# Output weights and bonus rows laid out for one-piece loads; the even layer's output projection in 256-token tiles with two sets of mixed inputs

## The chip, the cores and the metric

The kernel runs on one core of a Trainium2 chip. The metric is device microseconds (us) of one execution of the whole program; the profile is of one further execution. A core has five engines that run side by side and meet through semaphores: TensorE (PE in the profile, with its weight loads as PEld), VectorE (DVE), ScalarE (ACT), GpSimd (POOL) and SyncE (SP). SP issues all of this kernel's DMA transfers, in the order in which they stand in its instruction stream; the data are moved by the core's 16 DMA engines.

## The reference

A four-branch encoder trunk of one even and one odd layer, applied to a prompt of 1024 tokens and a sample of 2048 tokens, in float32. What matters here is the end of each layer:

```python
def even_layer(x, p):
    proj = rms_norm(x, p['norm']) @ p['w_in']
    u, z_s5, h_rw, z_rw = jnp.split(proj, [...], axis=-1)
    ya = s5_branch(u, z_s5, p)          # 512 columns, gated by silu(z_s5)
    yb = rwkv_branch(h_rw, z_rw, p)     # 512 columns
    return x + jnp.concatenate([ya, yb], -1) @ p['w_out']   # 1024 x 1024

def rwkv_branch(h, z, p):
    ...                                  # y: two scans, summed
    y = (y - mean) * rsqrt(var + RW_LN_EPS) * ln_g + ln_b   # per head of 64
    bonus = sum(r * k * r_k, -1, keepdims=True) * v         # per head of 64
    return (y + bonus) * silu(z)

def odd_layer(x, p):                     # windowed attention, gated
    return x + attn_branch(rms_norm(x, p['norm']) @ p['w_in'], p) @ p['w_out']
```

## The kernel before

The program has five stages, one after the other in time. `input_u` (to about 500 us) and `input_rkv` with `s5` (to about 1110 us) make the branch inputs; `input_rkv` also computes the bonus term and stores it to the DRAM tile `bon`. The recurrent mixers run to about 2270 us. Then one group of three phases follows: `even_out` (mixing, normalising and gating the two branches, the output projection, and x1 = x + result), `odd_in` (the odd layer's input projections) and `attention` (with the odd layer's output projection).

**even_out.** Work is in tiles of TT tokens: 256, 256, 512 for the prompt and four times 512 for the sample, seven tiles. The 1024 mixed inputs of a tile are eight blocks of 128 features. Blocks 0 to 3 are the S5 branch: `mix` (from DRAM tile `s5`) times the gate `zs`. Blocks 4 to 7 are the RWKV branch: per 128 tokens `yf` and `yr` are loaded (DRAM `y`), added, normalised; then for b = 0 to 3 the block is transposed by TensorE into PSUM `pt`, the bonus piece `bo` is loaded from `bon`, and two VectorE operations form (pt * ln_g + bo + ln_b) * zr. `emit` splits each block into a rounded part `mh[k]` (ScalarE) and a remainder `ml[k]` (VectorE). There is one set of `mh`/`ml` (pool `eom`, one buffer each), so a block of the next tile is written only after the projection of this tile has read it. The projection runs per 128 tokens and 512 output columns: 24 matmuls (8 blocks, three products each) into one PSUM buffer; then x is added and x1 stored. `bo` has two buffers, so the pieces for b = 2, 3 are asked for when those for b = 0, 1 have been used.

**Where the narrow shapes are.** `bon` is stored as [4, 2, 64, L], and a piece for b is `bon[2*(b%2):+2, 1-b//2, :, t0:t0+TT]`: two groups of 64 rows, whose DRAM side has the dimensions 2 x 64 x TT. The last four of the eight row blocks of `ev_w_out`, and all 16 pieces of `od_w_out` (eight row blocks, two column halves), are 2 x 64 rows of the weight in the same way. The SBUF side has 128 partitions each time.

**Order.** In this group, and in the two input groups, the code's operations are recorded with all their dependences (`Program.note`) and put into each engine's stream by a planner (`Program.put`): it keeps a clock for each engine, gives every operation a cost (a DMA by its bytes alone), and takes next what could start first, by rank. So a change of sizes or of the number of DMAs changes the order on every engine. All recorded operations carry line L412 in the profile; they are told apart by their operands: `ps<-sb` are the projections (also those of other phases of these groups), `ps<-ident,sb` are transposes, `sb<-bon` are the loads of bonus pieces, `x<-sb` the stores of x1. The mixers between have an order of their own.

Of the kernel before, what the change touches and what calls it, by code (L numbers as in the profile page):

```python
# [470 lines left out]
class Kern:  # L471
# [11 lines left out]
    T1, WP = 256, 2  # L483
# [214 lines left out]
    def input_rkv(self, st):  # L698
# [32 lines left out]
        for s, L in enumerate(self.L):  # L731
            t = self.sp[s]
            for t0 in range(0, L, self.seg):
# [37 lines left out]
                for p in range(4):  # L771
# [48 lines left out]
                    nc.sync.dma_start(t["bon"][p].rearrange("h r l -> (h r) l")[:, o0:o1], v)  # L820
# [916 lines left out]
    def even_out(self, st):  # L1737
        tc, nc, ins = self.tc, self.nc, self.ins
        cp = st.enter_context(tc.tile_pool(name="eoc", bufs=1))
        wo = ins["ev_w_out"][0]  # L1740

        turned_rows = lambda a: a.rearrange("(b h r) c -> h b r c", h=2, r=64)
        rows = [wo[P * k:P * k + P] for k in range(4)] + [turned_rows(wo[512:D])[1 - b // 2, 2 * (b % 2):2 * (b % 2) + 2] for b in range(4)]
# [3 lines left out]
        mp = st.enter_context(tc.tile_pool(name="eom", bufs=1))  # L1747
# [7 lines left out]
        for s, L in enumerate(self.L):  # L1755
            t = self.sp[s]
            sizes = [self.T1] * (512 // self.T1) if s == 0 else []
            sizes += [512] * (L // 512 - (s == 0))
            for t0, TT in zip(itertools.accumulate([0] + sizes), sizes):
                mh = [mp.tile([P, 512], F32R, name=f"mh{k}")[:, :TT] for k in range(8)]  # L1760
                ml = [mp.tile([P, 512], F32R, name=f"ml{k}")[:, :TT] for k in range(8)]
                zs, zr = (lp.tile([P, 4, 4, P], F32, name="z")[:, :TT // P] for _ in range(2))
                mix = [lp.tile([P, 4, 256], F32, name="mix") for _ in range(TT // 256)]
                for i in range(TT // 256):
                    nc.sync.dma_start(mix[i], t["s5"][t0 // 256 + i].rearrange("m c t -> c m t"))
# [8 lines left out]
                for m in range(4):  # L1774
                    out = mp.tile([P, 512], F32, name="smix", bufs=2)[:, :TT]
# [9 lines left out]
                for i in range(TT // P):  # L1785
# [11 lines left out]
                    yq = lp.tile([P, 512], F32, name="bo").rearrange("t (u v) -> t u v", v=64)  # L1797
# [93 lines left out]
    def attention(self, st):  # L1891
# [201 lines left out]
    def build(self):  # L2093
        tc = self.tc
        with ExitStack() as root:
# [14 lines left out]
          "rw_w_up", "rw_a0", "rw_a_up", "rw_k_k", "rw_k_a", "rw_r_k", "rw_ln_g", "rw_ln_b", "ev_w_out", "od_norm",  # L2110
          "od_w_in", "at_q_norm", "at_k_norm", "at_sink", "od_w_out"]


def _layout(inputs):
# [33 lines left out]
```

## Time and profile before

| | us |
|---|---|
| median of 3 runs | 4215.14 |
| lowest and highest | 4213.9 and 4220.34 |
| the profiled execution | 4222.45 |
| its span, first to last instruction | 4220.7 |
| even_out, from the end of the mixers to the last x1 | about 2270 to 2700 |
| PE busy over the whole span | 3795.9 (90%) |
| DVE busy | 2819.6 (67%) |
| ACT, POOL busy | 1933.0 (46%), 1611.2 (38%) |
| DMA: bytes moved | 570.30 MB, mean 135 GB/s |

The profiled execution is 7.3 us above the median. Busy shares are means over stages that differ, and matmuls are pipelined, so a busy PE need not be at its peak; the stage in which the change lies is read by itself. "PEclk" is the clock that TensorE was granted, as a part of 2.4 GHz (1.00 is 2.4 GHz, 0.50 is 1.2 GHz). The "DMA share" of a stretch is the mean over 16 DMA engines. In the chain of waits a piece named DMA is the time in which the last needed thing was a transfer.

### The profile page before, as it was taken

To read this page: it belongs to the slowest core of one execution; us is meant where nothing else is said; L and a number is where in the kernel's file an instruction comes from. 1 tells how busy PE (TensorE), PEld (TensorE's weight loads), DVE (VectorE), ACT (ScalarE), POOL (GpSimd) and SP (SyncE) were. 2 spreads that over 40 slices of the span, in tenths; PEclk is the share of its full clock that TensorE was granted. 3 is DMA by queue.
4 is the path that set the end of the run, shared out by engine and by line. 5 is a ranking of instruction groups with operands and counts; after the bars stand their busy time and mean duration, and the time that the engine had idled before them with its cause. 6 is when DMAs were issued, how large, how long until landed. Compare 5 with 4: busy or idle time off the path is not lost.

```text
span 4220.7 us, 87574 instructions
## 1 busy us (share of the span) xinstructions
PE 3795.9 (90%) x34128; PEld 3138.8 (74%) x34128; DVE 2819.6 (67%) x5513; ACT 1933.0 (46%) x4807; POOL 1611.2 (38%) x2007
## 2 busy tenths in 40 slices
PE   6878999999899999999996688899999979999999
PEld 4756766676788788888764466789999957878877
DVE  7356655656578888889873565444444449999997
ACT  3334333333345555656653111232333337777776
POOL 4422322222464554555511232122222225555554
PEclk9989999999999999999997789999999989999999
DMA  5576566656533343333443554444444422222221
GB/s 159 148 187 211 163 193 184 182 166 192 176 128 112 112 130 115 109 115 118 122 97 105 179 175 170 167 147 158 155 150 140 143 90 70 76 79 78 78 65 59
DMA packets 530946, 570.30 MB, mean 135 GB/s; under 512 B 92066, under 2 KB 430114, under 8 KB 519268
## 3 DMA queue, kind: packets, MB, share of 16 engines
q1 hardware_dynamic: 530532, 564.71, 43.6%
q8 instruction: 268, 4.39, 0.4%
q14 instruction: 146, 1.20, 0.1%
HBM read 398.03 MB, written 166.56 MB: 134 GB/s over the span
## 4 chain that ended last, share of the span: by engine, by line
PE 51%; DVE 16%; DMA 10%; issue 4%; POOL 3%; ACT 2%; SPq 1%; DVEq 0%; ACTq 0%; POOLq 0%
PE ps L412 36%; DVE sb L412 12%; PE acc L886 5%; DMA sb<-bon 3%; ACT sb L412 2%; PE pc L1332 2%; PE acc L969 2%; DMA sb<-wsp 2%; PE pg L1185 2%; POOL lt L1164 1%; DMA sb<-in_od_w_out 1%; DMA rk<-rk 1%; PE pY L1355 1%; PE pc L1319 1%; PE pc L1310 1%
## 5 line engine op out<-in xcount | busy, mean ns | idle before, releaser
L412 PE MATMUL ps<-sb 128*128 128x512 f32 (+8 forms) x12464 | 2563.8, 360 | 245.1 <-ACT sb L412 115.0
L412 PEld LDWEIGHTS ps<-sb 128*128 128x128 f32 (+2 forms) x12464 | 1975.6, 188 | 656.3 <-ACT sb L412 133.4
L412 POOL TENSOR_TENSOR sb<-sb,sb 128x384 f32<-128x384 f32 (+4 forms) x468 | 470.3, 1022 | 435.8 <-ACT sb L412 242.0
L412 POOL TENSOR_TENSOR sb<-sb 128x512 f32<-128x512 f32 (+5 forms) x358 | 316.4, 888 | 808.2 <-ACT sb L412 337.4
L412 DVE TENSOR_TENSOR sb<-ps,sb 128x512 fp32r<-128x512 f32 (+4 forms) x620 | 401.9, 661 | 226.3 <-PE ps L412 135.4
L412 ACT ACTIVATE sb<-sb 128x4 f32<-128x4 f32 (+7 forms) x352 | 269.4, 768 | 482.8 <-DVE sb L412 162.1
L412 POOL TENSOR_TENSOR sb<-sb,mhalf 128x8 f32<-128x8 f32 (+3 forms) x156 | 221.5, 1421 | 687.1 <-DVE sb L412 685.9
L886 PE MATMUL acc<-h,w 128*128 128x128 f32 x3072 | 450.4, 291 | 14.0 <-DMA w<-in_ev_w_zr 13.1
L886 PEld LDWEIGHTS acc<-h,w 128*128 128x128 f32 x3072 | 385.3, 197 | 39.5 <-POOL rt L1279 13.4
L412 PE MATMUL ps<-ident,sb 128*128 128x128 f32 x1888 | 316.0, 280 | 98.2 <-DVE sb L412 94.9
L412 ACT COPY sb<-ps 128x512 f32<-128x512 f32 (+4 forms) x402 | 194.9, 502 | 433.9 <-PE ps L412 419.3
L412 PEld LDWEIGHTS ps<-ident,sb 128*128 128x128 f32 x1888 | 236.8, 144 | 163.2 <-DVE sb L412 117.4
L412 DVE TENSOR_TENSOR sb<-sb,sb 128x512 fp32r<-128x512 f32 (+6 forms) x219 | 263.3, 1208 | 129.0 <-ACT sb L412 105.0
L412 ACT ACTIVATE sb<-sb,sb 128x384 f32<-128x384 f32 (+3 forms) x486 | 299.3, 619 | 108.8 <-DVE sb L412 58.4
L1164 POOL TENSOR_TENSOR lt<-rk,lb 64x256 f32<-64x256 f32 x288 | 216.2, 759 | 192.8 <-PE pY L1355 82.5
L1324 ACT COPY rt<-pc 32x128 f32<-32x128 f32 x768 | 196.8, 256 | 97.3 <-PE pc L1319 86.1
L412 DVE CUSTOM_DVE_ANT_0 sb<-ps,sb,sb 128x384 f32<-128x384 f32 (+1 forms) x384 | 215.4, 587 | 28.5 <-PE ps L412 25.3
L412 ACT ACTIVATE sb<-ps 128x512 f32<-128x512 f32 x108 | 64.4, 596 | 363.9 <-PE ps L412 355.4
L412 ACT CAST sb<-ps 128x512 fp32r<-128x512 f32 x368 | 202.0, 587 | 60.3 <-PE ps L412 57.5
L1149 POOL TENSOR_TENSOR kb<-rk,f 128x128 f32<-128x128 f32 x384 | 197.8, 547 | 82.5 <-PE pg L1195 68.8
L1339 DVE TENSOR_TENSOR rt<-pc,wc 64x256 f32<-64x256 f32 x376 | 158.3, 421 | 70.0 <-PE pc L1333 35.0
L412 DVE SCALAR_TENSOR_TENSOR sb<-sb,sb 128x512 f32<-128x512 f32 (+5 forms) x154 | 126.1, 826 | 117.0 <-ACT sb L412 112.8
(121 smaller groups left out, 4748.9 us busy)
## 6 DMA issues: line engine op xcount, KB each, us to landing
sb<-wsp SPq DMA_DIRECT2D x65, 1024.0 KB
rk<-rk SPq DMA_DIRECT2D x96, 512.0 KB
sb<-in_od_w_in SPq DMA_DIRECT2D x36, 1024.0 KB
h<-h SPq DMA_DIRECT2D x48, 512.0 KB
sb<-in_od_w_z SPq DMA_DIRECT2D x24, 1024.0 KB
qkv<-sb SPq DMA_DIRECT2D x72, 256.0 KB
sb<-qkv SPq DMA_DIRECT2D x72, 256.0 KB
sb<-in_x_sample SPq DMA_DIRECT2D x32, 512.0 KB
```

What stands on the lines that cost most here:

```text
L412: self.ops.append((eng, self.cost(eng, op, outs[-1] if outs[-1] is not k.get("accum_out") else outs[0], ins, a, k), deps, self.rank, lambd ...
L886: nc.tensor.matmul(sums[n][1][:, m * P:m * P + P], w[:, k, m * P:m * P + P], acts[n][0][:, k], start=k == 0, stop=k == KT - 1)
L969: nc.tensor.matmul(ps[:, 256 * (m % 2):256 * (m % 2) + 256], uw_at(k)[:, m], act_at(n)[:, 2 * k:2 * k + 2], start=k == 0, stop=k == 3)
L1149: nc.gpsimd.tensor_tensor(kb[:, sl, :, x, :], arr[n][:, sl, cs], f1[:, sl, cs, a:a + 32], MULT)
L1164: (nc.gpsimd if eng == "POOL" else nc.vector).tensor_tensor(ltv[:, :, :, at:at + 32], arr[n][rows, :, cs], f2[rows, :, cs, off:off + 32], ...
L1185: nc.tensor.matmul(g[64:P, c1, p], kb[0:64, p, c1].rearrange("c s i -> c (s i)"), lt[0:64, c1, 4 + p, 0:64], start=True, stop=True)
L1310: nc.tensor.matmul(pu[32 * q:32 * q + 32, j, :], lt[:, c1, u, 0:32], rt[:, c1, u, :], start=True, stop=True)
L1319: nc.tensor.matmul(pu[rows, 2 + j, :], win["tt"][d][0][rows, sys, :], u1[rows, j, :], start=True, stop=True, tile_position=(32 * q, 32 * q))
L1324: nc.scalar.copy(rt[rows, c1, 2 * q:2 * q + 2, :], pu[rows, 2:4])
L1332: nc.tensor.matmul(pu[0:64, 4 + p, :], lt[:, c1, 4 + p, 64:P], rt[:, c1, 4 + p, :], start=True, stop=True)
L1339: nc.vector.tensor_tensor(nrt[rows, n4 % 2, 4 - 4 * o:8 - 4 * o, :], pu[rows, 4:8], nh["wc"][rows, :, n4:n4 + 1].broadcast_to([64, 4, 64]) ...
L1355: nc.tensor.matmul(pY[32 * q:32 * q + 32, j, :], lt[:, c1, u, 32:64], rt[:, c1, u, :], start=True, stop=True)
```

## The change

The layouts that are made before the program runs now hold the two output weights with their rows in the order in which the kernel reads them (`ev_w_ot`, `od_w_ot`), so each block of 128 rows is one plain [128, columns] piece. `bon` becomes [2, 4, 64, L]; a loaded piece is then 128 rows with one stride, and a store of 128 rows becomes two stores of 64. In `even_out` every tile has 256 tokens (12 tiles), `mh` and `ml` have two buffers of 256 tokens where they had one of 512, the S5 mixing of a block is one VectorE operation on 256 tokens where it was one per 128, and the squares of the normalisation have a buffer `yq` of their own where they shared `bo`'s.

```diff
-            t["bon"] = dp.tile([4, 2, 64, L], F32, name=f"bon{s}")
+            t["bon"] = dp.tile([2, 4, 64, L], F32, name=f"bon{s}")
...
-                    nc.sync.dma_start(t["bon"][p].rearrange("h r l -> (h r) l")[:, o0:o1], v)
+                    for e in range(2):
+                        nc.sync.dma_start(t["bon"][e, p, :, o0:o1], v[64 * e:64 * e + 64])
...
     def even_out(self, st):
-        rows = [wo[P * k:P * k + P] for k in range(4)] + [turned_rows(wo[512:D])[1 - b // 2, 2 * (b % 2):2 * (b % 2) + 2] for b in range(4)]
+        rows = [ins["ev_w_ot"][P * k:P * k + P] for k in range(8)]
...
-        mp = st.enter_context(tc.tile_pool(name="eom", bufs=1))
+        mp = st.enter_context(tc.tile_pool(name="eom", bufs=2))
...
-            sizes = [self.T1] * (512 // self.T1) if s == 0 else []
-            sizes += [512] * (L // 512 - (s == 0))
-            for t0, TT in zip(itertools.accumulate([0] + sizes), sizes):
-                mh = [mp.tile([P, 512], F32R, name=f"mh{k}")[:, :TT] for k in range(8)]
-                ml = [mp.tile([P, 512], F32R, name=f"ml{k}")[:, :TT] for k in range(8)]
-                zs, zr = (lp.tile([P, 4, 4, P], F32, name="z")[:, :TT // P] for _ in range(2))
-                mix = [lp.tile([P, 4, 256], F32, name="mix") for _ in range(TT // 256)]
-                for i in range(TT // 256):
-                    nc.sync.dma_start(mix[i], t["s5"][t0 // 256 + i].rearrange("m c t -> c m t"))
+            TT = 256
+            for t0 in range(0, L, TT):
+                mh = [mp.tile([P, TT], F32R, name=f"mh{k}") for k in range(8)]
+                ml = [mp.tile([P, TT], F32R, name=f"ml{k}") for k in range(8)]
+                zs, zr = (lp.tile([P, TT // P, 4, P], F32, name=n) for n in ("zs", "zr"))
+                mix = lp.tile([P, 4, 256], F32, name="mix")
+                nc.sync.dma_start(mix, t["s5"][t0 // 256].rearrange("m c t -> c m t"))
...
-                    for i in range(TT // P):
-                        nat = lambda a: a.rearrange("c (n j) -> c j n", j=8)
-                        nc.vector.scalar_tensor_tensor(out=nat(out[:, P * i:P * i + P]), in0=mix[i // 2][:, m].rearrange("c (j n) -> c j n", j=8)[:, :, 16 * (i % 2):16 * (i % 2) + 16],
-                                                       scalar=0.25, in1=nat(zs[:, i, m]), op0=MULT, op1=MULT)
+                    nat = lambda a: a.rearrange("c i (n j) -> c i n j", j=8)
+                    nc.vector.scalar_tensor_tensor(out=nat(out.rearrange("c (i t) -> c i t", t=P)), in0=mix[:, m].rearrange("c (j i n) -> c i n j", j=8, i=2),
+                                                   scalar=0.25, in1=nat(zs[:, :, m]), op0=MULT, op1=MULT)
...
-                    yq = lp.tile([P, 512], F32, name="bo").rearrange("t (u v) -> t u v", v=64)
+                    yq = lp.tile([P, 8, 64], F32, name="yq")
...
-                    nc.sync.dma_start(bo, t["bon"][2 * (b % 2):2 * (b % 2) + 2, 1 - b // 2, :, t0:t0 + TT])
+                    nc.sync.dma_start(bo, t["bon"][1 - b // 2, 2 * (b % 2):2 * (b % 2) + 2, :, t0:t0 + TT].rearrange("b r l -> (b r) l"))
...
     # attention, weights(c)
-            v = ins["od_w_out"][0].rearrange("(k e g r) c -> k g e r c", e=2, g=4, r=64)
-            rows = [v[b // 4, b % 4] for b in range(8)]
+            rows = [ins["od_w_ot"][P * b:P * b + P, 512 * c:512 * c + 512] for b in range(8)]
```

Three places show how the instructions move. The first is SP at the start of `even_out`: the loads of the first tile and of the weights. Before:

```order
L412 DMA sb1_24256<-in_ev_w_out 128x1024 x3
L412 DMA sb1_24256<-y0_1_1_99 128x512
L412 DMA sb1_24256<-in_ev_w_out 128x1024
L412 DMA sb1_24256<-y0_0_2_92 128x512
L412 DMA sb1_24256<-y0_0_3_93 128x512
L412 DMA sb1_24256<-bon0_85 128x1x256
L412 DMA sb1_24256<-in_ev_w_out 128x1x1024 x4
L412 DMA sb1_24256<-y0_1_2_100 128x512
L412 DMA sb1_24256<-bon0_85 128x1x256
```

And now:

```order
L412 DMA sb1_24280<-bon0_85 128x256 x2
L412 DMA sb1_24280<-in_ev_w_ot 128x1024 x2
L412 DMA sb1_24280<-y0_0_2_92 128x512
L412 DMA sb1_24280<-y0_1_1_99 128x512
L412 DMA sb1_24280<-in_ev_w_ot 128x1024 x3
L412 DMA sb1_24280<-y0_0_3_93 128x512
L412 DMA sb1_24280<-in_ev_w_ot 128x1024
L412 DMA sb1_24280<-y0_1_2_100 128x512
L412 DMA sb1_24280<-in_ev_w_ot 128x1024 x2
```

The first two bonus pieces now stand ahead of the weights; none of the eight weight pieces is of the 2 x 64 form.

The second is PE in the steady part of `even_out`: `ps0` and `ps1` take the transposes of the RWKV blocks, `ps2` to `ps5` are the accumulators of the projection. Before, from the first transposes of a 512-token tile:

```order
L412 MATMUL ps0_24261<-ident_60,sb1_24256 128x128 x4
L412 MATMUL ps1_24262<-ident_60,sb1_24256 128x128 x4
L412 MATMUL ps2_24263<-sb2_24257 128x512 x6
L412 MATMUL ps0_24261<-ident_60,sb1_24256 128x128 x4
L412 MATMUL ps2_24263<-sb2_24257 128x512
L412 MATMUL ps1_24262<-ident_60,sb1_24256 128x128 x4
L412 MATMUL ps2_24263<-sb2_24257 128x512 x6
L412 MATMUL ps3_24264<-sb2_24257 128x512 x2
L412 MATMUL ps2_24263<-sb2_24257 128x512 x5
L412 MATMUL ps3_24264<-sb2_24257 128x512 x16
L412 MATMUL ps4_24265<-sb2_24257 128x512 x13
L412 MATMUL ps2_24263<-sb2_24257 128x512
```

And now, from the first transposes of a 256-token tile:

```order
L412 MATMUL ps0_24285<-ident_60,sb1_24280 128x128 x2
L412 MATMUL ps1_24286<-ident_60,sb1_24280 128x128 x2
L412 MATMUL ps2_24287<-sb2_24281 128x512 x5
L412 MATMUL ps0_24285<-ident_60,sb1_24280 128x128 x2
L412 MATMUL ps2_24287<-sb2_24281 128x512
L412 MATMUL ps1_24286<-ident_60,sb1_24280 128x128 x2
L412 MATMUL ps2_24287<-sb2_24281 128x512 x12
L412 MATMUL ps3_24288<-sb2_24281 128x512 x17
L412 MATMUL ps2_24287<-sb2_24281 128x512
L412 MATMUL ps3_24288<-sb2_24281 128x512 x2
L412 MATMUL ps4_24289<-sb2_24281 128x512
L412 MATMUL ps2_24287<-sb2_24281 128x512 x5
```

Between the last transposes of a tile and the first matmul that needs its seventh block (the single `ps2` row after the long ones) stood 42 matmuls, and stand 29 now.

The third is SP in the same steady part, around the second pair of bonus pieces of a tile. Before:

```order
L412 DMA sb1_24256<-zs1_2_195 128x2048
L412 DMA sb1_24256<-bon1_144 128x1x512 x2
L412 DMA sb1_24256<-in_x_sample 128x1024
L412 DMA sb1_24256<-y1_0_9_162 128x512
L412 DMA sb1_24256<-y1_0_10_163 128x512
L412 DMA sb1_24256<-y1_0_11_164 128x512
L412 DMA sb1_24256<-y1_0_12_165 128x512
L412 DMA sb1_24256<-zr1_2_191 128x2048
```

And now:

```order
L412 DMA x11_3_200<-sb1_24280 128x1024
L412 DMA sb1_24280<-y1_0_9_162 128x512
L412 DMA sb1_24280<-y1_0_10_163 128x512
L412 DMA sb1_24280<-bon1_144 128x256 x2
L412 DMA sb1_24280<-in_x_sample 128x1024
L412 DMA sb1_24280<-y1_1_10_179 128x512
L412 DMA sb1_24280<-zr1_2_191 128x1024
L412 DMA sb1_24280<-bon1_144 128x256 x2
```

The pair stands behind a store of x1 and two loads of y, and the next tile's first pair follows three loads later.

## Rows read from the trace of the kernel before

**Rows 1.** The page's part 4: the chain that ended last, shares by line

```profile
PE ps L412 36%; DVE sb L412 12%; PE acc L886 5%; DMA sb<-bon 3%; ACT sb L412 2%; PE pc L1332 2%; PE acc L969 2%; DMA sb<-wsp 2%; PE pg L1185 2%; POOL lt L1164 1%; DMA sb<-in_od_w_out 1%; DMA rk<-rk 1%; PE pY L1355 1%; PE pc L1319 1%; PE pc L1310 1%
```

**Rows 2.** Windows: stretch and us, each engine's busy time, PEclk, DMA share, GB/s

```profile
2270.00:2364.00 94.00, 31.28 (x110) 23.95 (x111) 33.55 (x62) 15.39 (x24) 16.14 (x27) 0.64 0.43 145
2364.00:2700.00 336.00, 272.05 (x1146) 217.41 (x1145) 185.92 (x334) 48.31 (x75) 89.66 (x66) 0.89 0.53 178
2700.00:3420.00 720.00, 701.09 (x4772) 650.85 (x4771) 312.77 (x388) 232.85 (x276) 179.17 (x143) 0.99 0.45 147
```

**Rows 3.** Windows: three short stretches of even_out, the columns of Rows 2

```profile
2280.00:2290.00 10.00, 3.87 (x9) 3.10 (x10) 7.62 (x16) 4.88 (x8) 3.79 (x3) 0.50 0.92 337
2310.00:2320.00 10.00, 0.69 (x2) 0.29 (x2) 1.83 (x2) 1.06 (x1) 0.00 (x0) 0.50 0.13 52
2491.07:2549.37 58.30, 48.11 (x209) 38.82 (x209) 33.73 (x61) 7.60 (x13) 17.02 (x13) 0.91 0.53 181
```

**Rows 4.** Timeline: start, us, engine; weight loads of even_out and their rounding

```profile
2284.89 0.38 SPq L412 DMA_DIRECT2D sb<-in_ev_w_out  x1
...
2288.88 22.94 SPq L412 DMA_DIRECT2D sb<-in_ev_w_out  x4
...
2290.72 1.06 ACT L412 ACTIVATE sb<-sb 128x1024 fp32r<-128x1024 f32 x1 [1.61 <-DMA sb<-in_ev_w_out]
...
2305.25 1.06 ACT L412 ACTIVATE sb<-sb 128x1024 fp32r<-128x1024 f32 x1 [8.86 <-DMA sb<-in_ev_w_out]
...
2336.59 1.06 ACT L412 ACTIVATE sb<-sb 128x1024 fp32r<-128x1024 f32 x1 [9.95 <-DMA sb<-in_ev_w_out]
```

**Rows 5.** Chain of waits: start, us, what; pieces in even_out

```profile
2321.77 18.95 DMA sb<-bon
...
2363.48 4.66 DMA sb<-y
...
2471.99 16.80 DMA sb<-bon
...
2491.07 30.19 PE ps L412 x122
...
2549.37 30.08 PE ps L412 x122
```

**Rows 6.** Timeline of one wait for a second pair of bonus pieces

```profile
2469.65 9.82 PE L412 MATMUL ps<-sb 128*128 128x512 f32 x42
...
2471.33 1.98 SPq L412 DMA_DIRECT2D sb<-bon  x2
...
2488.89 0.75 DVE L412 SCALAR_TENSOR_TENSOR sb<-ps,sb,sb 128x512 f32<-128x512 f32 x1 [4.88 <-DMA sb<-bon]
...
2491.07 34.94 PE L412 MATMUL ps<-sb 128*128 128x512 f32 x143 [11.60 <-ACT sb L412]
```

**Rows 7.** Timeline of PE: the first transposes of odd_in's first and second tile

```profile
2699.43 1.03 PE L412 MATMUL ps<-ident,sb 128*128 128x128 f32 x8
...
2835.49 1.03 PE L412 MATMUL ps<-ident,sb 128*128 128x128 f32 x8
```

**Rows 8.** Chain of waits: start of odd_in, and start of attention

```profile
2706.97 12.64 DMA sb<-in_od_w_out
...
3422.49 10.04 DMA sb<-in_od_w_out
...
3434.59 9.67 DMA z<-sb
3444.27 6.55 DMA sb<-qkv
...
3461.92 3.57 PE ps L412 x19
```

**Rows 9.** Tile bon: issue durations on SP, ns min/median/max

```profile
L412 SPq DMA_DIRECT2D bon<-sb x24: 319/332/469, 300.4 to 1107.6; - x24
```

**Rows 10.** The page's part 6: the split weights of the RWKV inputs, count and KB

```profile
sb<-wsp SPq DMA_DIRECT2D x65, 1024.0 KB
```

More of the change, by code (lines that the diff above doesn't have):

```diff
@@ L482 @@
     YF, YR = 5, 1
-    T1, WP = 256, 2
+    WP = 2
     RS, RW, RA = 10, 0, 0
@@ L1739, in even_out @@
         cp = st.enter_context(tc.tile_pool(name="eoc", bufs=1))
-        wo = ins["ev_w_out"][0]
-        turned_rows = lambda a: a.rearrange("(b h r) c -> h b r c", h=2, r=64)
-        rows = [wo[P * k:P * k + P] for k in range(4)] + [turned_rows(wo[512:D])[1 - b // 2, 2 * (b % 2):2 * (b % 2) + 2] for b in range(4)]
+        rows = [ins["ev_w_ot"][P * k:P * k + P] for k in range(8)]
         ln = cp.tile([P, 8], F32, name="ln")
@@ L1774, in even_out @@
                 for m in range(4):
-                    out = mp.tile([P, 512], F32, name="smix", bufs=2)[:, :TT]
-                    for i in range(TT // P):
-                        nat = lambda a: a.rearrange("c (n j) -> c j n", j=8)
-                        nc.vector.scalar_tensor_tensor(out=nat(out[:, P * i:P * i + P]), in0=mix[i // 2][:, m].rearrange("c (j n) -> c j n", j=8)[:, :, 16 * (i % 2):16 * (i % 2) + 16],
-                                                       scalar=0.25, in1=nat(zs[:, i, m]), op0=MULT, op1=MULT)
+                    out = mp.tile([P, TT], F32, name="smix")
+                    nat = lambda a: a.rearrange("c i (n j) -> c i n j", j=8)
+                    nc.vector.scalar_tensor_tensor(out=nat(out.rearrange("c (i t) -> c i t", t=P)), in0=mix[:, m].rearrange("c (j i n) -> c i n j", j=8, i=2),
+                                                   scalar=0.25, in1=nat(zs[:, :, m]), op0=MULT, op1=MULT)
                     emit(m, out)
@@ L1805, in even_out @@
                 for b in range(4):
-                    pt = pst.tile([P, 512], F32, name="pt")[:, :TT]
+                    pt = pst.tile([P, TT], F32, name="pt")
                     for i, y in enumerate(yn):
                         nc.tensor.transpose(pt[:, i * P:(i + 1) * P], y[:, b * P:(b + 1) * P], self.ident)
-                    bo = lp.tile([P, 512], F32, name="bo")[:, :TT]
-                    nc.sync.dma_start(bo, t["bon"][2 * (b % 2):2 * (b % 2) + 2, 1 - b // 2, :, t0:t0 + TT])
+                    bo = lp.tile([P, TT], F32, name="bo")
+                    nc.sync.dma_start(bo, t["bon"][1 - b // 2, 2 * (b % 2):2 * (b % 2) + 2, :, t0:t0 + TT].rearrange("b r l -> (b r) l"))
                     nc.vector.scalar_tensor_tensor(out=bo, in0=pt, scalar=lng[:, b:b + 1], in1=bo, op0=MULT, op1=ADD)
@@ L1907, in weights @@
         def weights(c):
-            v = ins["od_w_out"][0].rearrange("(k e g r) c -> k g e r c", e=2, g=4, r=64)
-            rows = [v[b // 4, b % 4] for b in range(8)]
-            return self.load_rows(cp, lp, [r[:, :, 512 * c:512 * c + 512] for r in rows], f"wo{c}", 0.5, (["wr"], 512, 2))
+            rows = [ins["od_w_ot"][P * b:P * b + P, 512 * c:512 * c + 512] for b in range(8)]
+            return self.load_rows(cp, lp, rows, f"wo{c}", 0.5, (["wr"], 512, 2))
         w = [weights(0)]
@@ L2109 @@
 _PLAIN = ["x_prompt", "x_sample", "ev_norm", "ev_w_in", "s5_log_dt", "s5_glu_w", "s5_glu_b", "rw_mu", "rw_w0",
-          "rw_w_up", "rw_a0", "rw_a_up", "rw_k_k", "rw_k_a", "rw_r_k", "rw_ln_g", "rw_ln_b", "ev_w_out", "od_norm",
-          "od_w_in", "at_q_norm", "at_k_norm", "at_sink", "od_w_out"]
+          "rw_w_up", "rw_a0", "rw_a_up", "rw_k_k", "rw_k_a", "rw_r_k", "rw_ln_g", "rw_ln_b", "od_norm",
+          "od_w_in", "at_q_norm", "at_k_norm", "at_sink"]
 def _layout(inputs):
@@ L2122, in _layout @@
     a["od_w_z"] = np.ascontiguousarray(np.asarray(inputs["od_w_in"])[0][:, 1536:].reshape(D, 2, 2, 4, 64).transpose(0, 1, 3, 2, 4).reshape(D, 1024))
+    wo = np.asarray(inputs["ev_w_out"])[0]
+    a["ev_w_ot"] = np.ascontiguousarray(np.concatenate([wo[:512], wo[512:].reshape(4, 2, 64, D).transpose(1, 0, 2, 3)[::-1].reshape(512, D)]))
+    a["od_w_ot"] = np.ascontiguousarray(np.asarray(inputs["od_w_out"])[0].reshape(2, 2, 4, 64, D).transpose(0, 2, 1, 3, 4).reshape(D, D))
     ln = [np.asarray(inputs[n])[0].reshape(2, 2, 2, 64)[:, :, ::-1] for n in ("rw_ln_g", "rw_ln_b")]
```

## The prediction

> **What bounds the kernel now.** I read the chain of waits by line first: TensorE's own rows lead it everywhere, but loads of the bonus pieces hold 3% of the span (some 125 us) and those of the odd output weight 1% [rows 1]. Both lie in places the change touches, so I cut the span there. From 2364 to 2700 us, the body of even_out, PE is busy 272.05 of 336 us at a granted clock of 0.89, and in the 94 us ahead of it 31.28 us at 0.64; odd_in after it runs at 701.09 of 720 and 0.99 [rows 2]. So even_out is where PE waits, and odd_in is full.
>
> For what it waits, the short stretches say. In 2280 to 2290 us the DMA engines move 337 GB/s at a share of 0.92; in 2310 to 2320 us only 52 GB/s at 0.13, which is two engines of 16, while nothing else is wanted but the four weight pieces of the 2 x 64 form [rows 3]. SP sits 22.94 us in issuing those four, and ScalarE rounds them one by one, from 2305.25 to 2336.59 us three intervals of 10.4 us [rows 4]. That is 512 KB by two engines. The bonus pieces have the same form. In the steady tile of 512 tokens PE runs out of work and stands 11.60 us, because the second pair of pieces, asked for at 2471.33, is first used up to its last piece at 2488.89 [rows 6]; the chain has 16.80 us for it, and one tile later PE starts again, 58.3 us on [rows 5]. In those 58.3 us PE is busy 48.11, VectorE 33.73, GpSimd 17.02, ScalarE 7.60 [rows 3]: no engine is full, the two DMA engines decide, and the clock (0.91, so part of the tile at 1.2 GHz) falls behind each wait.
>
> **The change part by part.** All durations are of the profiled execution (4222.45 us; its span is 4220.7), which is 7.3 us above the median.
>
> Start of even_out (window 2270 to 2364). The fourth weight piece, of the plain form, was issued at 2284.89 and rounded at 2290.72, 5.8 us later under full load [rows 4]. Plain, the other four move in 1.6 us each at 337 GB/s [rows 3]; the raw pieces have four buffers, so the last two wait for a rounding (1.06 us on ScalarE, about as much on VectorE) and another 5.8 us. From 2290.72 I add one such round, 8 us, and 2 us for the order: the last piece is rounded at about 2301 where it was at 2336.59, 35 us earlier. From there to the start of the y load at 2363.48, which follows the first tile's last store, took 27 us with two bonus waits in it (the longer one 18.95 us in the chain, begun earlier [rows 5]). With pieces that land as the 256 KB of y did, 4.66 us [rows 5], I allow 14: the pair 4.7 and its arithmetic 2.2, then 24 matmuls at half clock. Gain 35 + 13 = 48 us; bounds 35 (only the weights) and 55.
>
> Body of even_out. The matmuls stay: 192 per 512 tokens, and 16 transposes. At full clock 42 matmuls took 9.82 us [rows 6], 0.234 each, and eight transposes 1.03 us [rows 7]. A 256-token tile is 96 x 0.234 + 8 x 0.129 = 23.5 us of PE. What hides the rest: with two sets of mixed inputs the S5 blocks of the next tile are made while this one is projected. The RWKV blocks are not ahead by much: in the new order a tile's second pair of bonus pieces is still loaded under its own matmuls, and 29 of them cover it, 6.8 us, where 42 did (9.82). From landing to PE's restart took 2.18 us (2488.89 to 2491.07 [rows 6]); the issue came 1.2 us after the transposes or so (the pieces are half as wide now). So 6.8 - 1.2 - 2.2 = 3.4 us are left for landing. A plain piece of this size isn't in the trace: above it is the 4.66 us of y's 256 KB, below the 128 KB at 337 GB/s, 0.4 us; I take 4.66, since a 512 KB store and two y loads stand just ahead of the pair on SP. So each tile still waits 1.2 us: 24.7 us. The eleven tiles from 2364 to 2700 then take 272, and I add 5 for the second tile, whose order is not yet the steady one: 277 against 336, a gain of 59. Bounds: 11 x 23.5 = 258 with no wait (gain 78), and 11 x 28 with a landing of 8 us (gain 28).
> Does another engine stand in the way? VectorE's operations per 512 tokens go from 60 or so to 68: eight of the 128-token mixings merge, sixteen wider ones split in two. At its mean of 33.73/61 = 0.55 us the eight more make 38.1 us at most, of 49.4. The merged mixing reads `mix` with a larger stride than any row here; were it twice as slow per element, 4 x 0.5 us per tile would still fit. The bytes stay: 181 GB/s x 58.3 us is 10.6 MB per 512 tokens, in 49.4 us 214 GB/s, under the 337 seen [rows 3].
> The Trainium skill, "DMA: Bandwidth & Descriptors", section "Rules for kernel authors", speaks against the smaller tiles: it asks for transfers of 1 MiB or more and for few, large ones. In this trace 337 GB/s came with pieces of 256 and 512 KB [rows 3], and two engines limited, not the count; by its fixed cost of about 2 us a transfer (section "Anatomy of one DMA", given there for the GpSimd path) the 30 more transfers of even_out would be an estimated 60 us of latency, all of it in the way only if none overlapped. The sum above charges only the pair that is seen to be waited for.
>
> Start of odd_in. Its first tile takes 2699.43 to 2835.49, 136.1 us [rows 7]; the five others end at about 3422, 117.4 each. In the surplus of 18.7 us the chain names the odd output weight, 12.64 us [rows 8], which the same two engines carry beside x. The first tile also waits for its own weights and x1, which stay. I take 10; bounds 0 and 19.
>
> Start of attention. From 3422.49 to 3461.92 the chain is od_w_out 10.04, then a store of z 9.67 and a load of qkv 6.55 that stand behind it [rows 8]. Those three make 26.3 us; at 4.66 us each they would make 14.0, so 12.3 us less. I take 13, since the narrow pieces just before them go too; bounds 5 and 20.
>
> Stores of the bonus. 24 become 48, each 0.332 us of SP [rows 9], 8 us in all over some 800 us, among waits of SP. I cost them at nothing: the loads are issued ahead of their use. If that cover is gone they cost 8. The planner also makes a new order of the input stage around them; I take 0, from -8 to +8.
> The same section of the Trainium skill says of two transfers to disjoint partition halves: "Don't bother", use one 128-partition transfer. Here the halves go to different rows of `bon` for the sake of the load. No run shows the pair yet; by the rule the second store is pure extra, and at its 2 us this would be an estimated 48 us if each were waited for. No store of `bon` is among the lines of the chain [rows 1].
>
> Sum: 48 + 59 + 10 + 13 = 130. 4222.45 - 130 = 4092 for the profiled execution, 4085 on the median's footing; I forecast 4085. What is late next is PE itself in even_out, as in odd_in.
>
> **The rivals.**
> First: the second pair still holds every tile. It stands behind 512 KB of x1 and 512 KB of y, 3 us at 337 GB/s, so it may land after 9 us and not 4.66. Then each tile waits 5.6 us and takes 29.1: eleven take 320, the body gains 16, the sum is 87: 4128. For it: y's 4.66 us has no bytes listed ahead of it; against it: in the new order the store is issued early in the tile, before the pair's buffers are free.
> Second: the volume is the bound, not the two engines. If even_out can't pass the 181 GB/s of the steady tile [rows 3], the body gains nothing and the sum is 71: 4144. The 337 GB/s of the first stretch speaks against it.
> Third: the number of transfers. Twenty more bonus loads (28 become 48), each waited for at 4.66 us, give back 93: net 37, 4178. It would need each pair in turn to be late; the chain now shows mainly second pairs.
> Fourth: the loads stay narrow, so the change doesn't do what it says. Then the covers of 29 matmuls make each wait longer and the start stays: about as before, 4215. The new shapes in the order, 128x256 where 128x1x256 stood, speak against it.
> Fifth, slower: the input stage. Its 65 loads of split weights, 1 MB each [rows 10], hold 2% of the chain [rows 1], 84 us; SP's order there is planned anew round 24 more stores. If each of these loads comes 2.5 us later at a point where PE waits for it, that is +163 against -130: 4248. It decides from 2.0 us per load. Against it: 0.33 us of issue per store [rows 9].
>
> **How the numbers follow.** Forecast 0.70, first rival 0.12, second 0.06, third 0.04, fourth 0.03, fifth 0.03, and 0.02 for smaller mixtures that stay faster. The forecast's own terms span gains of 60 (35 + 28 + 0 + 5 - 8) to 180 (55 + 78 + 19 + 20 + 8), but hardly all at one end: 95 to 165 is likely, 4050 to 4120. I extend it to the first rival and a little over, 4140, and leave out the second to fifth: 4050 to 4140. A measurement of this kernel can tell 0.2%, 8 us, from no change. Faster by more than that: all but the fourth and fifth, 0.94; within it: the fourth, 0.03; slower: the fifth, 0.03.
>
> **What would show it.** In the new profile the rounding of even_out's weights should end near 2301 us on the old scale and no stretch of even_out should stand at 0.13 DMA share; bonus loads should leave the front of the chain; PE should restart every 25 us at a granted clock near 1.00, with x1's last store some 105 us earlier; odd_in's first tile should take about 126 us, and attention begin about 27 us after odd_in. Wrong would be: tiles of 28 us or more with a wait on `sb<-bon` in each (first rival), GB/s that stays at 180 with DMA share near 0.9 (second), or an input stage that ends later than 1107 us by tens (fifth).

## The result and the profile after

| us | before | after |
|---|---|---|
| median, 4 runs each | 4217.74 | 4063.43 |
| lowest and highest | 4213.9 to 4223.13 | 4061.16 to 4065.39 |
| profiled execution (span) | 4222.45 (4220.7) | 4065.39 (4063.7) |

The ratio of after to before is 0.9633, interval 0.9616 to 0.965: 154 us faster. The forecast was 4085, with a range of 4050 to 4140.

The chain of waits of after, by line, against [rows 1]:

```profile
PE ps L412 30%; DVE sb L412 11%; PE acc L887 5%; PE pc L1333 2%; PE acc L970 2%; PE pg L1186 2%; ACT sb L412 2%; DMA rk<-rk 1%; DVE ng L1251 1%; DVE z L1253 1%; PE pY L1356 1%; PE pc L1320 1%; POOL lt L1165 1%; PE pc L1311 1%; DVE lt L1206 1%
```

The bonus loads (3%) and the odd output weight (1%) are gone from the leading lines. So are the split weights `sb<-wsp` (2%), but that is no gain: PE's waits on them between 300 and 1100 us are 23.2 us in both profiles. For the stages I cut each profile at the same four events. A runs from even_out's first issue on SP to the second x1 store of its first 256 tokens, B from there to odd_in's first transposes, C to those of odd_in's second tile, and the rest to the end of the span.

| profile | A begins | A | B | C | rest |
|---|---|---|---|---|---|
| before | 2272.8 | 91.5 | 335.1 | 136.1 | 1385.2 |
| after | 2272.0 | 46.8 | 260.5 | 117.0 | 1367.4 |
| difference | -0.8 | -44.7 | -74.6 | -19.1 | -17.8 |

Windows of after (stretch and us; busy time of PE, PEld, DVE, ACT, POOL; granted clock, DMA share, GB/s), against [rows 2, 3]:

```profile
2272.00:2318.80 46.80, 30.30 (x119) 23.06 (x119) 37.78 (x60) 16.12 (x27) 19.89 (x28) 0.78 0.90 309
2318.80:2579.30 260.50, 251.93 (x1131) 204.05 (x1130) 180.89 (x367) 54.78 (x113) 87.96 (x65) 0.99 0.68 230
2280.00:2290.00 10.00, 4.13 (x12) 3.33 (x13) 8.83 (x14) 4.95 (x8) 5.03 (x4) 0.56 1.01 380
2290.00:2300.00 10.00, 9.07 (x42) 7.01 (x40) 9.54 (x11) 5.94 (x7) 6.47 (x4) 1.00 0.86 284
2300.00:2310.00 10.00, 8.34 (x30) 5.80 (x29) 9.93 (x20) 3.21 (x9) 1.26 (x1) 0.83 0.94 325
```

The body of even_out is now full of TensorE work, 251.93 of 260.50 us, at a clock of 0.99 where it was 0.89, and at 230 GB/s where it was 178. In A the mean DMA share is 0.90; the stretch at 0.13 is gone, and of all stretches of 10 us from 2270 to 2580 us none has a share under 0.40.

PE's waits in B, by what ended them (us in total, times, the longest), of before and then of after:

```profile
PE ps L412 <- ACT sb L412: 57.0, 8, 11.6
PE ps L412 <- DVE sb L412: 7.0, 9, 3.5
```

```profile
PE ps L412 <- DVE sb L412: 4.5, 2, 2.8
PE ps L412 <- ACT sb L412: 4.0, 7, 0.7
```

ScalarE is only the last link there: it rounds the block that waited for a bonus piece. The waits fell from 64.0 to 8.5 us, 55.5 less. The rest of B's gain, some 19 us, is PE's own busy time, 271.21 us in the same cut of before, for the same matmuls at the higher clock. The end of before's wait of 11.60 us ([rows 6]) and what came behind it, in the columns of the windows, shows both:

```profile
2486.00:2488.00 2.00, 0.00 (x0) 0.00 (x0) 0.00 (x0) 0.00 (x0) 0.00 (x0) 0.50 0.13 51
2488.00:2490.00 2.00, 0.00 (x0) 0.00 (x0) 1.11 (x2) 0.00 (x0) 0.00 (x0) 0.50 0.13 51
2491.07:2495.00 3.93, 3.92 (x9) 2.77 (x10) 3.93 (x7) 1.25 (x2) 1.02 (x1) 0.50 0.76 272
2500.00:2505.00 5.00, 5.00 (x24) 4.13 (x23) 3.38 (x7) 0.63 (x1) 4.12 (x4) 1.00 0.45 156
```

The wait ends at two engines' share and 51 GB/s. Then PE does 9 matmuls in 3.92 us at a granted clock of 0.50, and 24 in 5.00 us once it is at 1.00. A wait for data was thus paid twice, as idle time and as clock.

ScalarE's roundings of the weights (start, us), against [rows 4]:

```profile
2290.58 1.06 ACT L412 ACTIVATE sb<-sb 128x1024 fp32r<-128x1024 f32 x1 [0.23 <-DMA sb<-in_ev_w_ot]
...
2295.99 1.06 ACT L412 ACTIVATE sb<-sb 128x1024 fp32r<-128x1024 f32 x1 [0.77 <-DMA sb<-in_ev_w_ot]
...
2299.07 1.06 ACT L412 ACTIVATE sb<-sb 128x1024 fp32r<-128x1024 f32 x1 [2.01 <-DMA sb<-in_ev_w_ot]
```

The last begins at 2299.07, where it began at 2336.59. One wait for a second pair, in the timeline (SP, PE and VectorE), against [rows 6]:

```profile
2488.73 6.85 PE L412 MATMUL ps<-sb 128*128 128x512 f32 x29
...
2489.81 0.86 SPq L412 DMA_DIRECT2D sb<-bon  x2
...
2493.94 0.48 DVE L412 SCALAR_TENSOR_TENSOR sb<-ps,sb,sb 128x256 f32<-128x256 f32 x1 [3.89 <-DMA sb<-bon]
2494.75 0.48 DVE L412 SCALAR_TENSOR_TENSOR sb<-ps,sb,sb 128x256 f32<-128x256 f32 x1 [0.33 <-DMA sb<-bon]
...
2496.13 14.13 PE L412 MATMUL ps<-sb 128*128 128x512 f32 x61 [0.55 <-ACT sb L412]
```

The 29 matmuls of the new order cover the pair, and PE stands 0.55 us instead of 11.60. The chain of waits there, against [rows 5]:

```profile
2466.46 4.63 DMA sb<-bon
...
2472.57 9.38 PE ps L412 x40
...
2490.24 4.42 DMA sb<-bon
...
2496.13 9.38 PE ps L412 x40
...
2513.66 3.95 DMA sb<-bon
...
2519.08 60.84 PE ps L412 x276
```

Bonus pieces are still on the chain of the body, seven of them at 2.46 to 4.63 us where one was 16.80, and none behind the last one shown. PE restarts after 23.56 us (2472.57 to 2496.13) and 22.95 (to 2519.08). Odd_in's first tile, against [rows 7], takes 117.0 us:

```profile
2579.31 1.03 PE L412 MATMUL ps<-ident,sb 128*128 128x128 f32 x8
...
2696.31 1.03 PE L412 MATMUL ps<-ident,sb 128*128 128x128 f32 x8
```

At the start of attention, PE's waits in 145 us (before 3415 to 3560, after 3280 to 3425), of before and then of after:

```profile
PE ps L412 <- ACT sb L412: 14.5, 3, 13.6
PE ps L412 <- POOL sb L412: 12.9, 3, 10.9
PE ps L412 <- DVE sb L412: 10.3, 17, 1.4
```

```profile
PE ps L412 <- DVE sb L412: 11.5, 21, 2.1
PE ps L412 <- ACT sb L412: 1.6, 1, 1.6
PE ps L412 <- POOL sb L412: 1.5, 2, 0.8
```

The two long waits, behind the transfers of [rows 8], are gone: 37.7 us became 14.6.

### The profile page after: what moved, and what is told of

It is laid out like the page before. It is cut to its first block, busy times and chain, and to the rows that moved or that the text cites. A ratio compares the mean times of both kernels' runs of the same rounds, so it can differ in the third digit from the quotient of the medians.

```text
span 4063.7 us, 87721 instructions
## 1 busy us (share of the span) xinstructions
PE 3763.6 (93%) x34128; PEld 3118.4 (77%) x34128; DVE 2821.8 (69%) x5545; ACT 1939.8 (48%) x4847; POOL 1615.8 (40%) x2007
## 3 DMA queue, kind: packets, MB, share of 16 engines
q1 hardware_dynamic: 535908, 564.72, 45.4%
## 4 chain that ended last, share of the span: by engine, by line
PE 45%; DVE 17%; DMA 4%; issue 4%; POOL 3%; ACT 2%; SPq 1%; DVEq 0%; ACTq 0%; POOLq 0%
PE ps L412 30%; DVE sb L412 11%; PE acc L887 5%; PE pc L1333 2%; PE acc L970 2%; PE pg L1186 2%; ACT sb L412 2%; DMA rk<-rk 1%; DVE ng L1251 1%; DVE z L1253 1%; PE pY L1356 1%; PE pc L1320 1%; POOL lt L1165 1%; PE pc L1311 1%; DVE lt L1206 1%
## 5 line engine op out<-in xcount | busy, mean ns | idle before, releaser
L412 POOL TENSOR_TENSOR sb<-sb,sb 128x384 f32<-128x384 f32 (+5 forms) x468 | 469.5, 1021 | 444.2 <-ACT sb L412 226.0
L412 ACT ACTIVATE sb<-sb 128x256 fp32r<-128x256 f32 (+9 forms) x392 | 276.1, 710 | 286.3 <-DVE sb L412 128.5
L412 PE MATMUL ps<-ident,sb 128*128 128x128 f32 x1888 | 317.2, 280 | 55.5 <-DVE sb L412 51.1
L412 DVE TENSOR_TENSOR sb<-sb,sb 128x256 fp32r<-128x256 f32 (+6 forms) x259 | 265.8, 1038 | 142.9 <-ACT sb L412 128.8
L412 DVE TENSOR_SCALAR sb<-sb,sb 128x384 f32<-128x384 f32 (+4 forms) x264 | 190.6, 751 | 18.2 <-POOL sb L412 16.2
```

The source lines that it names most:

```text
L412: self.ops.append((eng, self.cost(eng, op, outs[-1] if outs[-1] is not k.get("accum_out") else outs[0], ins, a, k), deps, self.rank, lambd ...
```

## The experiments

Eleven kernels ran, in four groups on the chip, each group beside the kernel before (its medians there 4229 to 4236). So kernels are compared by their ratio to before, and stages within a profile. In the nine of these profiles whose bonus stores are of plain rows A begins at 2277 to 2284 us.

| kernel | ratio, interval | A begins | A | B | C | rest |
|---|---|---|---|---|---|---|
| after | 0.9633 [0.9616, 0.965] | 2272.0 | 46.8 | 260.5 | 117.0 | 1367.4 |
| wide_only | 0.9654 [0.9631, 0.9677] | 2277.0 | 45.7 | 270.1 | 117.0 | 1366.7 |
| tiles_only | 0.9984 [0.9971, 0.9998] | 2282.8 | 90.6 | 336.9 | 129.8 | 1381.2 |
| narrow_bon | 0.985 [0.9822, 0.9877] | 2278.3 | 56.5 | 334.5 | 117.0 | 1367.3 |
| one_set | 0.9632 [0.9609, 0.9656] | 2284.4 | 46.7 | 259.5 | 116.9 | 1366.3 |
| narrow_ev | 0.9703 [0.9673, 0.9733] | 2282.6 | 80.4 | 262.3 | 117.0 | 1367.5 |
| narrow_od | 0.9683 [0.9661, 0.9706] | 2283.6 | 47.1 | 260.9 | 129.6 | 1383.3 |
| groups | 0.9691 [0.9669, 0.9713] | 2280.3 | 77.9 | 265.2 | 117.0 | 1366.8 |
| bo4 | 0.959 [0.9572, 0.9609] | 2281.8 | 45.4 | 258.1 | 117.0 | 1354.7 |
| pad | 0.9612 [0.9594, 0.9629] | 2284.2 | 47.5 | 261.6 | 117.0 | 1356.6 |
| one_store | 0.9742 [0.972, 0.9764] | 2329.0 | 47.5 | 264.5 | 117.0 | 1368.3 |
| cut_store | 0.9666 [0.965, 0.9683] | 2301.0 | 47.2 | 260.1 | 117.0 | 1368.4 |

The theory: two groups of 64 rows put a transfer on two DMA engines, and the layouts, which take this away, are the whole gain. The rival: the tiles of 256 tokens and the second set of mixed inputs are a large part of it.

**wide_only**: the layouts alone (the edit against before, in words).

```diff
+ ev_w_ot, od_w_ot, bon [2, 4, 64, L] with its two stores
  tiles of 256, 256, 512, ... tokens, one set of mh/ml, as before
```

> The new layouts and nothing else: seven tiles (256, 256, five of 512), one set of mixed inputs, 128-token mixing. Theory (the 2 x 64 form confines a transfer to two DMA engines, and that is what even_out waited for): nearly all of the gain. The tile's 11.6 us wait goes, since 42 matmuls (9.82 us) cover a landing of 4.2 us, and the clock rises with it: about 46.5 us per 512 tokens, total 4070 to 4085. Rival (the smaller tiles and the second set made the gain): most of the wait stays because one set of mixed inputs serialises the tiles: body gains under 20 us, total 4120 or more.

The layouts alone hold nearly all the gain; the intervals of the two ratios overlap. B is 9.6 us longer than in after, 49.1 us per 512 tokens and not 46.5. Two of the loads that its first 512-token tiles wait for, in the chain of waits:

```profile
2357.68 8.06 DMA sb<-zs
...
2406.93 6.78 DMA sb<-zs
```

**tiles_only**: the other half alone (the edit against before, in words).

```diff
+ tiles of 256 tokens, two sets of mh/ml, yq
  ev_w_out, od_w_out, bon [4, 2, 64, L], as before
```

> 256-token tiles with two sets, all loads in the old 2 x 64 form. Theory: little gain, since the pairs of bonus pieces still take the two engines 5 us each pair of 128 KB, with less work to hide them (29 matmuls, 6.8 us): 27 to 30 us per tile, start and attention as before: 4180 to 4215. Rival (tiles and sets made the gain): 4120 or less.

Even less than the theory had left it: B is that of before. Its waits there:

```profile
PE ps L412 <- ACT sb L412: 53.1, 11, 6.5
PE ps L412 <- DVE sb L412: 6.6, 3, 2.5
```

Half-size pieces make shorter waits (6.5 us at most, not 11.6) and more of them (11, not 8); the two engines carry the same bytes. The rival falls.

**narrow_bon**: after, with the bonus rows in the old layout.

```diff
-            t["bon"] = dp.tile([2, 4, 64, L], F32, name=f"bon{s}")
+            t["bon"] = dp.tile([4, 2, 64, L], F32, name=f"bon{s}")
...
-                    for e in range(2):
-                        nc.sync.dma_start(t["bon"][e, p, :, o0:o1], v[64 * e:64 * e + 64])
+                    nc.sync.dma_start(t["bon"][p].rearrange("h r l -> (h r) l")[:, o0:o1], v)
...
-                    nc.sync.dma_start(bo, t["bon"][1 - b // 2, 2 * (b % 2):2 * (b % 2) + 2, :, t0:t0 + TT].rearrange("b r l -> (b r) l"))
+                    nc.sync.dma_start(bo, t["bon"][2 * (b % 2):2 * (b % 2) + 2, 1 - b // 2, :, t0:t0 + TT])
```

> The changed kernel with the old bonus layout (loads in the 2 x 64 form, one store of 128 rows); weights plain. Theory: each of the 12 tiles waits about 5 us more for its second pair and the first tile about 8 more: 4120 to 4145. Rival (the bonus was hidden by the two sets): 4065 to 4075.

It costs more than expected, because the whole gain of B is given back (334.5 us), and 9.7 us of A. The body of narrow_bon (columns as in the windows above):

```profile
2334.80:2669.30 334.50, 277.95 (x1136) 223.10 (x1135) 178.64 (x367) 55.02 (x113) 87.84 (x65) 0.89 0.55 179
```

Clock and GB/s are those of before.

**one_set**: after, with one set of mixed inputs.

```diff
-        mp = st.enter_context(tc.tile_pool(name="eom", bufs=2))
+        mp = st.enter_context(tc.tile_pool(name="eom", bufs=1))
...
-                    out = mp.tile([P, TT], F32, name="smix")
+                    out = mp.tile([P, TT], F32, name="smix", bufs=2)
```

> The changed kernel with one set of mixed inputs of 256 tokens (and still two buffers for the S5 product). Theory: the blocks of the next tile are made while the last accumulator of this one still runs, block by block, so PE waits 1 to 2 us at each of 11 tile ends: 4072 to 4090. Rival (the second set is what lets PE run on): 5 us or more per tile, 4115 or more.

B is 259.5 us, not longer at all, against both expectations: the second set is worth nothing here.

**narrow_ev** and **narrow_od**: after, with one output weight in the old row order.

```diff
-        rows = [ins["ev_w_ot"][P * k:P * k + P] for k in range(8)]
+        rows = [wo[P * k:P * k + P] for k in range(4)] + [turned_rows(wo[512:D])[...] for b in range(4)]
...
-            rows = [ins["od_w_ot"][P * b:P * b + P, 512 * c:512 * c + 512] for b in range(8)]
+            v = ins["od_w_out"][0].rearrange("(k e g r) c -> k g e r c", e=2, g=4, r=64)
+            rows = [v[b // 4, b % 4] for b in range(8)]
...
```

> The changed kernel with the even output weight read as before (four of eight row blocks in the 2 x 64 form). Theory: only the start of even_out: the last of the four is rounded 35 us later, as in the kernel before, less what the early bonus pieces save: 4090 to 4100. Rival (the weights' loads were hidden): under 4070.

A becomes 80.4, 33.6 us longer, with the old picture in it (two engines' share while ScalarE rounds one piece):

```profile
2310.00:2320.00 10.00, 0.00 (x0) 0.00 (x0) 1.23 (x1) 1.06 (x1) 0.00 (x0) 0.68 0.13 52
```

> The changed kernel with the odd output weight read as before (16 pieces in the 2 x 64 form). Theory: the first tile of odd_in takes 19 us longer (136 against 117) and attention starts 18 us later, as in the kernel before: 4095 to 4103. By my forecast's terms (10 and 13): 4086. Rival (what odd_in's first tile and the attention gained came from the other parts of the change): under 4072.

C is 12.6 and the rest 15.9 us longer, where 19 and 18 were expected. At the start of narrow_od's attention the chain of waits names the weight, piece after piece:

```profile
3301.61 10.22 DMA sb<-in_od_w_out
...
3313.30 10.18 DMA sb<-in_od_w_out
...
3324.89 12.04 DMA sb<-in_od_w_out
```

Taken together, narrow_ev and narrow_bon give back 43.3 of the 44.7 us of A, narrow_bon 74.0 of the 74.6 of B, and narrow_od 12.6 of the 19.1 of C and 15.9 of the 17.8 of the rest: 146 of 157 us, each layout in its own place.

**groups**: is it the number of groups or the distance between the rows? The even weight is read in 4 groups of 32 rows, the odd one in 16 of 8, both with the rows apart.

```diff
+    a["ev_w_ot"] = ...reshape(8, 4, 32, D).transpose(1, 0, 2, 3)     # a piece: [:, k]
+    a["od_w_ot"] = ...reshape(8, 16, 8, D).transpose(1, 0, 2, 3)     # a piece: [:, b, :, columns]
```

> The changed kernel with the weights' rows laid apart in DRAM: every block of the even weight as 4 groups of 32 rows, every piece of the odd weight as 16 groups of 8 rows. Theory (the number of engines is that of the outer groups): the even weight's eight blocks go by four engines, 5.1 us each, 41 us in a row: 20 to 30 us later at the start, DMA share near 0.25 there and about 104 GB/s; the odd weight's pieces use 16 engines and cost nothing: 4083 to 4095 in all, odd_in's first tile 117 us. Rival (pieces are slow because their rows lie apart): the odd weight costs 37 us as in the 2 x 64 form, the even weight 35 or more: 4130 or more.

Sixteen groups cost nothing (C and the rest as in after), four cost 31 us in A. Two stretches during the weight loads of groups:

```profile
2295.00:2300.00 5.00, 1.62 (x4) 1.33 (x5) 1.64 (x2) 1.58 (x2) 0.00 (x0) 0.50 0.26 104
2315.00:2320.00 5.00, 3.96 (x10) 3.13 (x11) 1.99 (x3) 1.55 (x3) 1.64 (x1) 0.50 0.26 104
```

A share of 0.26 is 4 engines of 16, and 104 GB/s is twice 52, both as expected. All eight pieces on four engines cost about what four pieces on two do (77.9 and 80.4 us). The number of groups decides, not that the rows lie apart.

**bo4** and **pad**: after, with four bonus buffers instead of two, so that a second pair can be asked for before the first is used; and after with the same room, unused.

```diff
-                    bo = lp.tile([P, TT], F32, name="bo")
+                    bo = lp.tile([P, TT], F32, name="bo", bufs=4)
```

```diff
+        pad = lp.tile([P, 256], F32, name="pad")
```

> The changed kernel with four buffers for bonus pieces, so that all four of a tile can be loaded ahead. Theory: the waits of 0.3 to 0.75 us for the second pair in six tiles go, and some of the second and third tile's: 4056 to 4061. Rival (PE holds the body already, or the landing isn't what the second pair waits for): no change within 0.1%, 4063.

A and B are 1.4 and 2.4 us shorter, within the 2 to 7 us expected, but the rest is 12.7 us shorter, which nothing in the expectation explains.

> The changed kernel with an unused buffer of 2 x 128 x 256 f32 beside the bonus buffers of even_out: nothing is computed or moved with it, it only shifts where later buffers lie, and with that the planned order of attention. Theory (bo4's 12.7 us in attention came from placement and order, not from earlier bonus loads): even_out's body stays as in the changed kernel (258 to 262 us, PE waiting some 4 us on ScalarE there), and the part after odd_in's first tile drops from 1367 to 1352-1362; ratio to before 0.959 to 0.962. Rival (four bonus buffers in use are needed for it): body 260, the rest 1366 to 1369, ratio 0.963.

The unused room gives 10.8 of the 12.7 us. In the traces PE's instructions from odd_in to the end of attention stand in the same order in pad and bo4, and in another one in after. The traces of one_set, narrow_bon, narrow_ev, groups and one_store have after's order, and their rest is 1366.3 to 1368.3 us. So the gain belongs to an order: the room shifts where later buffers lie, and the planner made another order. (The ratios of pad and after have intervals that overlap; the stages tell them apart.) The 150 us that begin 850 us after odd_in's first transposes, of after and then of pad:

```profile
3429.30:3579.30 150.00, 141.55 (x818) 115.89 (x819) 136.86 (x354) 112.57 (x306) 84.61 (x110) 0.99 0.24 76
```

```profile
3443.30:3593.30 150.00, 145.22 (x850) 121.31 (x851) 138.89 (x367) 116.25 (x319) 88.66 (x114) 1.00 0.27 83
```

32 more matmuls are done in it. bo4 is the fastest kernel that ran (4060.4 us beside 4236.2 of before), most of its advantage by luck of placement.

**one_store** and **cut_store**: after, with each bonus block stored at once, 2 x 64 rows; and in two halves of its tokens, 2 x 64 rows each.

```diff
-                    for e in range(2):
-                        nc.sync.dma_start(t["bon"][e, p, :, o0:o1], v[64 * e:64 * e + 64])
+                    nc.sync.dma_start(t["bon"][:, p, :, o0:o1], v)
```

```diff
+                    oh = (o1 - o0) // 2
                     for e in range(2):
-                        nc.sync.dma_start(t["bon"][e, p, :, o0:o1], v[64 * e:64 * e + 64])
+                        nc.sync.dma_start(t["bon"][:, p, :, o0 + oh * e:o0 + oh * e + oh], v[:, oh * e:oh * e + oh])
```

> The changed kernel, but each bonus store is again one transfer of 2 x 64 rows (328 KB at most) instead of two of 64. Theory (the outer group count sets the engines): the 24 stores move by two engines at 52 GB/s, some 6 us each where the two halves take under 2; whatever stands behind them on those two engines in the input stage comes later: even_out starts 5 to 20 us later in the profile, the rest as in the changed kernel, ratio 0.964 to 0.968. Rival (a store that nobody waits for may be slow, and one transfer is cheaper to issue than two): even_out starts 0 to 8 us earlier, ratio 0.961 to 0.963.

A begins 45 us later than in pad, which ran beside it, more than twice what was expected. The planner's order isn't the reason. In the traces SP's 805 and PE's 4432 instructions of the input stage stand in the same order in one_store as in before, tiles_only and narrow_bon, which make the same 24 stores with 128 plain rows, and in these A begins at 2272.8 to 2282.8 us, 46 to 56 us earlier. PE's waits in the input stage (300 to 1100 us), of narrow_bon and then of one_store:

```profile
PE ps L412 <- DMA sb<-wsp: 20.2, 9, 5.9
...
PE ps L412 <- ACT sb L412: 9.3, 10, 1.7
```

```profile
PE ps L412 <- DMA sb<-wsp: 35.0, 9, 7.3
PE ps L412 <- ACT sb L412: 23.4, 13, 3.9
```

The weights of the RWKV inputs come later. At the end of the stage the stores are waited for themselves: SP's first instruction of the mixers (L1003) stands behind the last one, of narrow_bon and then of one_store:

```profile
SPq L1003 <- DMA bon<-sb: 1.2, 1, 1.2
```

```profile
SPq L1003 <- DMA bon<-sb: 7.7, 1, 7.7
```

> The changed kernel, but the two stores of each bonus block are cut by tokens and not by halves of the rows: 48 stores of the same bytes as in the changed kernel, each of 2 x 64 rows of half the tokens. Theory (one_store lost 45 us ahead of even_out because its stores go by two engines): the number is that of the changed kernel, the engines are two again, so even_out starts 30 to 60 us later than the changed kernel's, ratio 0.971 to 0.978. Rival (one_store lost it by its new order of the input stage or by the number of stores, not by the engines): even_out starts within 15 us of the changed kernel's, ratio 0.961 to 0.966.

A begins at 2301.0, 17 to 24 us later than in the nine profiles with plain stores: between the two expectations, neither of which holds. Cut into windows of 1 us, the input stage (300 to 1200 us) has 44 with a DMA share of 0.10 to 0.15 and 44 to 58 GB/s in one_store and 46 in cut_store, and 2 to 4 in before, after, tiles_only, narrow_bon and pad. So the stores of both kernels take two engines, for about as long. The chain of cut_store has its last store in front of the mixers:

```profile
1125.98 7.88 DMA bon<-sb
```

Why cut_store loses only about half as much stays open. Its stores are half as long, and its order of the input stage is neither that of one_store nor that of after.

## Why the prediction was right, and where its sizes were off

The mechanism held: two engines behind the waits that went, PE as the next bound in the body. The sum was 130 us and 157 came, by the profiled executions.

- **Start of even_out**: 48 forecast, 44.7 measured. Two misses nearly cancel in it. The last weight was rounded 2 us before the forecast (about 2301; 2299.07). From there to the first tile's end it took 19.7 us and not 14: from 2300 to 2321 us 93% of the chain are VectorE's operations (9.93 us busy of 10 in the window from 2300 shown above), and the forecast had asked about VectorE only for the body.
- **Body**: 59 forecast, 74.6 measured, near the upper bound of 78. The term mis-sized most is the wait per tile. The landing was priced nearly rightly (4.66; 2.46 to 4.63 us on the chain), but fewer tiles than all eleven waited for it. From the second piece's use to PE's restart took 1.38 us and not 2.18, since the operations have half the width (0.48 us where one took 0.75), and all waits of B are 8.5 us where 11 x 1.2 + 5 = 18.2 were allowed. PE itself needed 251.9 us, not 258.5. Taking y's row as the landing was right; taking the old tile's tail unscaled was not.
- **First tile of odd_in**: 10 forecast, 19.1 measured, the upper bound. I let half of its surplus stay for its own weights and x1. Nothing of it stayed; narrow_od brings back 12.6. The 6.5 us between are gone in tiles_only too (C 129.8): either edit removes them, so the two don't add.
- **Start of attention**: 13 forecast, 17.8 measured, within its bounds; narrow_od brings back 15.9.
- **Bonus stores**: 0 forecast, 0.8 us measured, well inside the spread of the start of A: with one and the same order of the input stage it is 2272.0 us in after and 2284.2 in pad. SP pays 48 x 0.561 us for them, not 48 x 0.332; that is some 19 us more than before, and A begins no later. SP's issues in after, against [rows 9]:

```profile
L412 SPq DMA_DIRECT2D bon<-sb x48: 473/561/1597, 298.9 to 1100.1; - x48
```

- **The second set**: I let it hide the S5 blocks. one_set shows that it hides nothing; the argument for the tile time didn't need it.

Of the rivals, the first (9 us of landing), the second (181 GB/s as a bound; 230 came) and the third (the number of transfers) fall by the rows of after. The fourth is tiles_only, at 0.9984, as priced. The fifth, an input stage that is late by its weight loads, didn't happen with stores of 64 plain rows: the last of them was issued at 1100.1 us, before it was 1107.6. But one_store shows its mechanism in the same place: there A begins 45 us late, and PE's waits on these loads are 14.8 us longer than with plain stores in the same order.

On the rule of the Trainium skill against two transfers to partition halves ("DMA: Bandwidth & Descriptors", section "Rules for kernel authors"): here the pair of stores cost nothing measurable, and one store in two groups cost 45 us. The same page, section "Why a DMA increments its semaphore by 16 and not by 1", says that the slowest dimension above 1 of the access patterns sets how many engines a transfer uses; 2 groups at a share of 0.13, 4 at 0.26, and 16 without cost agree with it. The advice of 1 MiB per transfer, in "Rules for kernel authors", was not needed: A of after reached 380 GB/s with pieces of 128 to 512 KB.

## What to carry to other kernels

Look for stretches in which the DMA share is a simple fraction (0.13 is 2 of 16, 0.26 is 4) while something waits, and then at the outermost dimension of the transfers there; here a layout made once, ahead of the program, cured it. Look in short windows: over the whole body of before the share was 0.53, and only pieces of a wait stood at 0.13. Judge a store by what stands behind it on its engines and by the first instructions of the next stage, not only by whether anyone waits for it in its own. And where a planner orders the program, run a version that only shifts the buffers before crediting an edit with ten microseconds.

## What the runs showed of the hardware

- Loads of 2 x 64 rows moved at 52 GB/s with a DMA share of 0.13 (before, 2310 to 2320 us), loads of 4 x 32 rows at 104 GB/s with 0.26 (groups), so some 26 GB/s per engine; plain pieces reached 380 GB/s with 1.01 (after).
- The clock followed the waits: the same matmuls of B took 271.2 us of PE at a granted clock of 0.89 with waits of up to 11.6 us between them, and 251.9 us at 0.99 with none over 2.8. Behind a wait of 11.60 us PE began at 0.50.
- Issuing a store of 64 rows took SP 0.561 us in the median of 48 (0.506 in pad), one of 128 plain rows 0.332, one of 2 x 64 rows 0.534 (one_store): the halves were not cheaper to issue.
- Stores in the 2 x 64 form made the stage after them start 46 to 56 us later than the same stores of 128 plain rows, in the same order on SP and PE.
